# A Winograd convolution on one core: half of a late image stored by GpSimd's queue, one separate slice of rows given up, the first store issued by ScalarE

## The chip, the core and the metric

The kernel runs on one core of a Trainium2 chip. The metric is the device time in microseconds (us), the median of several runs. Lower is better. One further execution was profiled; all durations below come from it.

## The reference

A 3x3 convolution with padding 1 over 16 images of 64 channels and 64 x 64 pixels, giving 128 channels, all in float32:

```python
x_pad = np.pad(x, ((0, 0), (0, 0), (1, 1), (1, 1)), mode='constant')
# for every b, co, ci, kh, kw:
output[b, co] += weight[co, ci, kh, kw] * x_pad[b, ci, kh:kh+h, kw:kw+w]
```

The input x has 16.8 MB, the output 33.6 MB.

## The kernel before

Two images make a pair: their 2 x 64 input channels fill the 128 partitions. There are 8 pairs, p = 0 to 7, and each is worked in two halves of 32 output rows, h = 0 and 1 (line 185). GpSimd makes the Winograd row sums and differences of a half two steps ahead (line 206). TensorE multiplies (lines 216 to 228), ScalarE copies partial sums out of PSUM and casts input rows, and VectorE and ScalarE write the finished rows of the half into an output tile (lines 229 to 232).

Inputs and outputs live in nine slots of one tile, `homes`. Each slot holds one 2 MB block: the input of a pair, or one image of an output pair, in which each of the 128 partitions has 16 KB, one output channel. `X_HOME` and `O_HOME` (lines 49, 50) say which slots a pair takes. A slot is used again once the transfer that reads it has landed and the engines that read it are through.

All DMA transfers are issued from SyncE's queue (SP), in program order: the weights (line 58), the inputs of pairs 0 to 4 at the start (lines 68 to 72, pairs 3 and 4 in one transfer of 4 MB), then stores and the loads of pairs 5 to 7 in turn (lines 234 to 236). `store(p, both)` runs after the second half of a pair:

- for the pairs in `BOTH = (0, 3, 6)`, one transfer of 4 MB with both images (line 190);
- for the others, one transfer of 2 MB for each image (line 199);
- with `FEW = 5, 1, 7`, the second image of pair 5 goes in three: 57 rows of all 128 channels, and the last 7 rows as one transfer of 124 channels and one of 4 (lines 194 to 196).

`keep` holds the instructions of an engine in the order in which they are written. GpSimd has no compute after the transforms of the last half, and it issues no DMA.

Of the kernel before, what the change touches and what calls it, by code (L numbers as in the profile page):

```python
# [15 lines left out]
def kernel(  # L16
# [12 lines left out]
    nc = tc.nc  # L29
    B, CI, H, W = x.shape  # L30
    CO = weight.shape[0]
# [4 lines left out]
    keep = tc.keep_in_program_order  # L36
# [11 lines left out]

    X_HOME = [0, 1, 2, 7, 8, 2, 7, 8]
    O_HOME = [5, 3, 0, 5, 3, 0, 5, 2]  # L50
    BOTH = (0, 3, 6)
    FEW = 5, 1, 7
    NEXT_LOADS = {(2, 0): 5, (3, 0): 6, (4, 0): 7}
    homes = slots.tile([128, 9, H, W], F32)
    xs = [homes[:, k, :, :] for k in X_HOME]
# [4 lines left out]
    def load(p, cuts=((0, H),)):  # L60
        for lo, hi in cuts:
            keep(
                nc.sync.dma_start(
                    xs[p][:, lo:hi, :], x_rows[128 * p : 128 * p + 128, lo:hi, :]
                )
            )
# [55 lines left out]
    def cast(p, h):  # L122
        t = cpool.tile([128, 17, W], F16, tag="xh", name="xh")
        keep(nc.scalar.copy(t, xs[p][:, C_ROW[h] : C_ROW[h] + 17, :]))  # L124
        return t

    def transforms(eng, p, h):
        return sums(eng, p, h), diffs(eng, p, h), outers(eng, p, h)
# [17 lines left out]
    def mms(tiles, terms, start, stop):  # L146
        n = 3 * len(terms)
        i = 0
        for wi, src, row in terms:
            for kw in (1, 0, 2):  # L150
                c_lo, c_hi = max(0, 1 - kw), min(W, W + 1 - kw)
                lo, hi = 0, RB
                at, step, rows = row
                while at + step * lo < 0:
                    lo += 1
                while at + step * (hi - 1) > rows - 1:
                    hi -= 1
                first, last = at + step * lo, at + step * (hi - 1)
                for b2 in range(2):
                    p0 = 64 * b2  # L160
                    keep(
                        nc.tensor.matmul(  # L162
                            tiles[:, b2, lo:hi, c_lo:c_hi],
                            Wt[p0 : p0 + 64, wi, kw, :],
                            src[
                                p0 : p0 + 64,
                                first : last + 1 : step,
                                c_lo + kw - 1 : c_hi + kw - 1,
                            ],
                            start=start and i == 0,  # L170
                            stop=stop and i == n - 1,
                            skip_group_check=not start,
                        )
                    )
                i += 1

    def acc():
        return psum.tile([128, 2, RB, W], F32, tag="acc", name="acc")

    def copied(tiles):  # L180
        ut = upool.tile([128, 2, RB, W], F32, tag="ut", name="ut")
        keep(nc.scalar.copy(ut, tiles))  # L182
        return ut
# [3 lines left out]
    def store(p, both):  # L187
        if p in BOTH:
            pair = out[2 * p : 2 * p + 2, :, :, :].rearrange("b c h w -> c b h w")
            keep(nc.sync.dma_start(pair, both))  # L190
            return
        for b2 in range(2):
            parts = [(0, CO, 0, H)]
            if (p, b2) == FEW[:2]:
                at = H - FEW[2]
                parts = [(0, CO, 0, at), (0, 124, at, H), (124, 4, at, H)]
            for c, n, lo, hi in parts:
                keep(
                    nc.sync.dma_start(
                        out[2 * p + b2, c : c + n, lo:hi, :], both[c : c + n, b2, lo:hi, :]  # L200
                    )
                )

    for n, (p, h) in enumerate(halves):
        if n + 2 < len(halves):
            tr[halves[n + 2]] = transforms(nc.gpsimd, *halves[n + 2])
        if h == 0:
            both = homes[:, O_HOME[p] : O_HOME[p] + 2, :, :]
            ov = both.rearrange("p b (j i) c -> p b j i c", i=2)
        ss, dd, ee = tr.pop((p, h))  # L210
        xc = xh.pop((p, h))
        jf, jg = RB * F_BLK[h], RB * G_BLK[h]
        sf, sg = jf - 16 * h, jg - 16 * h
        g_at = 2 * jg - C_ROW[h]

        pf1, pg1, pf2, pg2 = acc(), acc(), acc(), acc()
        mms(pf1, [(HP, ss, (sf, 1, 16))], True, True)
        ux = copied(pf1)
        mms(pg1, [(G1, ss, (sg, 1, 16))], True, True)
        ug = copied(pg1)  # L220
        mms(pf2, [(HM, dd, (0, 1, RB))], True, True)
        uy = copied(pf2)
        if n + 1 < len(halves):
            xh[halves[n + 1]] = cast(*halves[n + 1])
        mms(pg2, [(G01, xc, (g_at, 2, 17)), (G2, xc, (g_at + 2, 2, 17))], True, True)
        mms(pf1, [(G0, ee, (0, 2, 16))], False, True)
        mms(pg1, [(G21, xc, (g_at + 1, 2, 17)), (G0, xc, (g_at - 1, 2, 17))], False, True)
        mms(pf2, [(G2, ee, (1, 2, 16))], False, True)
        keep(nc.vector.tensor_add(ov[:, :, jg : jg + RB, 1, :], pg2, ug))  # L229
        keep(nc.vector.tensor_add(ov[:, :, jf : jf + RB, 0, :], pf1, uy))  # L230
        keep(nc.vector.tensor_sub(ov[:, :, jf : jf + RB, 1, :], ux, pf2))  # L231
        keep(nc.scalar.copy(ov[:, :, jg : jg + RB, 0, :], pg1))  # L232
        if h == 1:
            store(p, both)
        if (p, h) in NEXT_LOADS:
            load(NEXT_LOADS[p, h])
# [30 lines left out]
```

## Time and profile before

| what | value |
|---|---|
| median of 3 runs | 127.05 us (126.71 to 127.71) |
| the profiled execution | 126.84 us |
| its span, from first to last instruction | 125.0 us |
| TensorE busy | 96.3 us (77%), done by 103.5 us |
| GpSimd, ScalarE, VectorE busy | 90.5, 81.5, 64.3 us |
| moved by DMA | 50.77 MB, mean 406 GB/s |
| HBM read, written | 17.07 MB, 33.55 MB |

The span is the stretch that the profile shows; the profiled execution's own time has some 1.8 us around it. In the profile PE is TensorE, DVE VectorE, ACT ScalarE, POOL GpSimd and SP SyncE; a "q" behind the name is the engine's issuing sequencer. Slices are fortieths of the span, 3.1 us each, and a digit is the busy share in tenths. L199 is line 199 of the kernel. The trace also has a record of each DMA packet, with its queue, its size, its start and its duration; a packet of 4 bytes is the count that a DMA engine adds to a semaphore when its part of a transfer is done. The records do not say which of the 16 DMA engines carried a packet.

### The profile page before, as it was taken

How to read it: one execution, taken by the hardware profiler on the slowest of the kernel's cores; microseconds unless marked ns; L12 is line 12 of the kernel's file. 1: busy time of each engine (PE TensorE's matmuls, PEld its weight loads, DVE VectorE, ACT ScalarE, POOL GpSimd, SP SyncE). 2: the span in 40 equal slices, each digit the busy share in tenths (PEclk: the TensorE clock that was granted, in tenths of full speed). 3: DMA queues.
4: the chain of work that ended last, by engine and by line, in shares of the span. 5: the costliest groups of instructions: out<-in, count | busy, mean ns of one | idle time of the engine just before them, and what ended most of it. 6: DMA issues, size and time to landing. Idle time of an engine off the chain costs nothing.

```text
span 125.0 us, 2161 instructions
## 1 busy us (share of the span) xinstructions
PE 96.3 (77%) x873; PEld 48.3 (39%) x873; DVE 64.3 (51%) x56; ACT 81.5 (65%) x86; POOL 90.5 (72%) x52
## 2 busy tenths in 40 slices
PE   0339999999999999999999999999999991000000
PEld 0213455554545545554545555545545540000000
DVE  0199484655738393947557483939374664000000
ACT  4456569789897979797888989797978842000000
POOL 2209999999999999999999999999999500000000
PEclk9999999999999999999999999999999999555555
DMA  4999999999999999999999999999999999999991
GB/s 126 364 433 440 430 430 430 425 346 404 430 425 419 440 430 440 406 425 425 432 438 398 430 425 425 435 430 425 430 419 428 428 421 431 435 425 440 430 388 63
DMA packets 3826, 50.77 MB, mean 406 GB/s; under 512 B 360, under 2 KB 488, under 8 KB 744
## 3 DMA queue, kind: packets, MB, share of 16 engines
q1 hardware_dynamic: 3816, 50.63, 96.6%
q8 instruction: 7, 0.11, 0.3%
q14 instruction: 3, 0.02, 0.1%
HBM read 17.07 MB, written 33.55 MB: 405 GB/s over the span
## 4 chain that ended last, share of the span: by engine, by line
PE 77%; DVE 3%; DMA 3%; POOL 1%; ACT 0%; issue 0%; DVEq 0%
PE acc L162 76%; DMA w_raw<-in_weight_dram 3%; DVE homes L231 1%; DVE ss L106 1%; POOL w L78 1%; DVE th L133 0%; DVE Wt L134 0%; PE wp L95 0%; ACT g0h L131 0%; DVEq L134 0%
## 5 line engine op out<-in xcount | busy, mean ns | idle before, releaser
L162 PEld LDWEIGHTS <-Wt 64*128 64x128 f16 x864 | 47.4, 96 | 50.0 <-issue 4.4
L182 ACT COPY ut<-acc 128x1024 f32<-128x1024 f32 x48 | 45.7, 1021 | 5.5 <-PE acc L162 5.5
L162 PE MATMUL acc<-xh,Wt 64*128 64x504 f16 (+3 forms) x384 | 46.9, 376 | 0.0
L106 POOL TENSOR_TENSOR ss<-homes 128x1024 f16<-128x1024 f32 x15 | 35.3, 2352 | 5.0 <-DMA homes<-in_x_dram 5.0
L229 DVE TENSOR_TENSOR homes<-acc,ut 128x1024 f32<-128x1024 f32 x16 | 19.6, 1225 | 32.4 <-PE acc L162 30.2
L119 POOL TENSOR_TENSOR ee<-homes 128x1024 f16<-128x1024 f32 x15 | 35.4, 2359 | 0.0
L162 PE MATMUL acc<-ss,Wt 64*128 64x504 f16 (+1 forms) x192 | 24.8, 392 | 2.4 <-DVE ss L106 2.4
L162 PE MATMUL acc<-ee,Wt 64*128 64x504 f16 (+1 forms) x192 | 26.3, 377 | 0.0
L232 ACT COPY homes<-acc 128x1024 f32<-128x1024 f32 x16 | 16.2, 1013 | 12.7 <-PE acc L162 12.0
L231 DVE TENSOR_TENSOR homes<-ut,acc 128x1024 f32<-128x1024 f32 x16 | 19.5, 1221 | 2.0 <-PE acc L162 1.3
L113 POOL TENSOR_TENSOR dd<-homes 128x512 f16<-128x512 f32 x15 | 20.0, 1332 | 0.0
L230 DVE TENSOR_TENSOR homes<-acc,ut 128x1024 f32<-128x1024 f32 x16 | 19.4, 1215 | 0.0
L124 ACT CAST xh<-homes 128x1088 f16<-128x1088 f32 x16 | 17.9, 1120 | 0.0
L162 PE MATMUL acc<-dd,Wt 64*128 64x504 f16 (+1 forms) x96 | 13.9, 392 | 0.0
L95 PE MATMUL wp<-ident,w 128*128 128x128 f16 x9 | 1.1, 309 | 4.8 <-POOL w L78 4.8
L133 DVE SCALAR_TENSOR_TENSOR th<-wp,g0h 128x384 f32<-128x384 f32 x1 | 0.6, 557 | 5.8 <-ACT g0h L131 5.8
L119 DVE TENSOR_TENSOR ee<-homes 128x1024 f16<-128x1024 f32 x1 | 2.9, 2866 | 0.0
L95 PEld LDWEIGHTS <-w 128*128 128x128 f16 x9 | 0.9, 158 | 4.7 <-POOL w L78 4.7
L78 POOL CAST w<-w_raw 128x576 f16<-128x576 f32 x1 | 0.7, 662 | 2.7 <-DMA w_raw<-in_weight_dram 2.7
L79 ACT CAST w<-w_raw 128x576 f16<-128x576 f32 x1 | 0.7, 671 | 1.9 <-DMA w_raw<-in_weight_dram 1.9
L79 ACT ACT_TABLE_LOAD x1 | 1.3, 1283 | 0.7 <-PEq L251 0.7
L106 DVE TENSOR_TENSOR ss<-homes 128x1024 f16<-128x1024 f32 x1 | 1.2, 1224 | 0.0
(15 smaller groups left out, 5.7 us busy)
## 6 DMA issues: line engine op xcount, KB each, us to landing
out_dram<-homes SPq DMA_DIRECT2D x9, 2048.0 KB, 16.7
out_dram<-homes SPq DMA_DIRECT2D x3, 4096.0 KB, 21.2
homes<-in_x_dram SPq DMA_DIRECT2D x5, 2048.0 KB, 19.0
homes<-in_x_dram SPq DMA_DIRECT2D x1, 4096.0 KB, 28.0
out_dram<-homes SPq DMA_DIRECT2D x1, 1824.0 KB, 22.6
homes<-in_x_dram SPq DMA_DIRECT2D x1, 1088.0 KB, 5.8
homes<-in_x_dram SPq DMA_DIRECT2D x1, 960.0 KB, 7.8
w_raw<-in_weight_dram SPq DMA_DIRECT2D x1, 288.0 KB, 3.2
```

The lines of the kernel that those rows point to most:

```text
L79: keep(nc.scalar.copy(w16[:, 1, :], w_raw))
L95: keep(nc.tensor.matmul(wps[kh][:, k * CO : k * CO + CO], w16[:, :, 3 * kh + k :: 9], ident))
L106: keep(eng.tensor_add(t, v[:, j : j + 16, 0, :], v[:, j : j + 16, 1, :]))
L113: keep(eng.tensor_sub(t, v[:, j : j + RB, 1, :], v[:, j : j + RB, 0, :]))
L119: keep(eng.tensor_sub(t, xs[p][:, r - 1 : r + 15, :], xs[p][:, r + 1 : r + 17, :]))
L124: keep(nc.scalar.copy(t, xs[p][:, C_ROW[h] : C_ROW[h] + 17, :]))
L162: nc.tensor.matmul(tiles[:, b2, lo:hi, c_lo:c_hi], Wt[p0 : p0 + 64, wi, kw, :], src[p0 : p0 + 64, first : last + 1 : step, c_lo + kw - 1 : ...
L182: keep(nc.scalar.copy(ut, tiles))
L229: keep(nc.vector.tensor_add(ov[:, :, jg : jg + RB, 1, :], pg2, ug))
L230: keep(nc.vector.tensor_add(ov[:, :, jf : jf + RB, 0, :], pf1, uy))
L231: keep(nc.vector.tensor_sub(ov[:, :, jf : jf + RB, 1, :], ux, pf2))
L232: keep(nc.scalar.copy(ov[:, :, jg : jg + RB, 0, :], pg1))
```

## The change

Four things change. The second image of pair 5 goes in one transfer, without the separate rows. Pair 3 leaves `BOTH` and goes as two transfers of one image each. Pair 0's store is issued by ScalarE in place of SyncE. For the last pair's first image, the upper 32 rows of channels 0 to 122 are issued by GpSimd, 3 channels (120 to 122) and then 120 (0 to 119), as soon as the pair's first half is computed; SyncE issues the same rows of the other 5 channels and then the lower 32 rows of all 128 after the second half, as before, and the second image after that.

```diff
-    BOTH = (0, 3, 6)
-    FEW = 5, 1, 7
+    BOTH = (0, 6)
+    SOFT = 7, 0, 32
...
-            keep(nc.sync.dma_start(pair, both))
+
+            eng = nc.scalar if p == 0 else nc.sync
+            keep(eng.dma_start(pair, both))
             return
         for b2 in range(2):
             parts = [(0, CO, 0, H)]
-            if (p, b2) == FEW[:2]:
-                at = H - FEW[2]
-                parts = [(0, CO, 0, at), (0, 124, at, H), (124, 4, at, H)]
+            if (p, b2) == SOFT[:2]:
+                parts = [(123, 5, 0, SOFT[2]), (0, CO, SOFT[2], H)]
...
+    def soft_store(p, both):
+
+
+        b2, hi = SOFT[1:]
+        for c, n in ((120, 3), (0, 120)):
+            keep(
+                nc.gpsimd.dma_start(
+                    out[2 * p + b2, c : c + n, 0:hi, :], both[c : c + n, b2, 0:hi, :]
+                )
+            )
...
         keep(nc.scalar.copy(ov[:, :, jg : jg + RB, 0, :], pg1))
+        if (p, h) == (SOFT[0], 0):
+            soft_store(p, both)
         if h == 1:
             store(p, both)
```

## The prediction

> **What bounds the kernel now.** I read the page's slices first, then the chain of waits, then SP's own waits and the timeline around each store, and last the DMA packet records.
>
> ```profile
> PE   0339999999999999999999999999999991000000
> ...
> DMA  4999999999999999999999999999999999999991
> GB/s 126 364 433 440 430 430 430 425 346 404 430 425 419 440 430 440 406 425 425 432 438 398 430 425 425 435 430 425 430 419 428 428 421 431 435 425 440 430 388 63
> ...
> q1 hardware_dynamic: 3816, 50.63, 96.6%
> q8 instruction: 7, 0.11, 0.3%
> ```
>
> TensorE is done after two thirds of the row; the DMA engines are full from the second slice to the last but one. Bytes over rate make the time: 50.63 MB at the usual 430 GB/s are 117.7 us of the 125.0 us span. The dent of 346 and 404 is in slices 8 and 9 (25 to 31 us).
>
> ```profile
> 8.31 95.19 PE acc L162 x864
> 103.50 0.02 issue
> 103.52 1.22 DVE homes L231
> ```
>
> The chain of waits ends with the last output tile at 104.74 us. SP issues the last two transfers then, and nothing but DMA is left:
>
> ```profile
> 24.26 0.39 SPq L190 DMA_DIRECT2D out_dram<-homes  x1
> ...
> 93.30 0.40 SPq L190 DMA_DIRECT2D out_dram<-homes  x1
> 104.80 1.92 SPq L199 DMA_DIRECT2D out_dram<-homes  x2
> ```
>
> At 104.80 us pair 6's 4 MB are still under way; its 16 parts land from 111.2 to 114.5 us. So compute has some 6 us of cover, and the end is set by the slowest of 16 DMA engines.
>
> Which engine that is can be rebuilt. An engine starts a packet 4 ns before the end of the one before is put down, and a 16 KB packet takes 611 ns, so the records string into 16 chains. Their last packets end at 120.5, 120.7, 121.0, 121.4, 122.1, 122.2, 122.3, 122.35, 122.4, 122.8, 123.1 (two), 123.3, 123.5, 123.6 and 123.9 us; the last count is seen 0.3 us later, at 124.2, and 0.8 us of closing instructions follow. The mean is 122.4: perfect balance would give 1.5 us, no more. Seven chains each carry one instruction packet (q8, some 0.95 us); the last chain has the first of them and besides a packet of 2089 ns in the dent. Four chains carry pair 5's 7 separate rows: 32 packets of 1792 bytes each. They end at 122.8, 123.1, 123.5 and 123.6; the last chain is none of the four.
>
> **The change part by part.** *Separate rows given up.* The four chains lose 32 packets at 74 ns less 3.5 overlap (2.26 us) and get 8 packets of 611 in place of 545 ns (0.53): 1.73 us less. The twelve others get 0.53 us more, among them the last one. Whatever else happens, the last chain goes from 123.9 to 124.4: **+0.53 us**, unless it is relieved. Two issues on SP fall away; SP waits for outputs, so that is nothing.
>
> *The half image on GpSimd's queue.* The transfer of 124 channels gives the nearest row for how channels spread: its packets lie in four chains, 31 channels each, and 4 is the largest divisor of 124 up to 16. (The 360 four-byte packets agree: 22 transfers with 16 counts, two with 4.) Read in that way, 120 channels go over 15 engines, 8 each, 3 over three and 5 over five. A packet of 8 KB, between 7680 bytes (291 ns) and 8704 (328), is 310 ns, net 306. Fifteen engines carry the same load as now (16 times 306 against 8 times 607: +0.04); the sixteenth is spared 8 times 306 = 2.45 us; some get one or two packets more, +0.31 each. What it does to the end depends on which engine is spared. If the last one: the next are those at 123.3 and 123.1, which end at 123.9 and 123.7, so −0.02 us in all. If any other: +0.57. The trace before has no transfer from GpSimd and the records name no engines, so both ends stay in the range. I take +0.57: fifteen engines of sixteen give it.
>
> [...]
>
> *Its timing.* The rows are final at 99.04 us (VectorE's L231 starts at 97.82 and takes 1.22). GpSimd's last work ends at 98.8, so nothing queues behind the two issues but the closing drain. Their making has no row; SP's take 0.33 to 1.5 us each. Against that stand 12 us until pair 6's parts land: nothing. The transfer takes turns with pair 6's packets, which land some 2.4 us later; nobody waits for them. If the second half's writes to the same slot waited for the transfer, the last issue would slip by some 8 us past its 6 us of cover; but pair 0's first half started at 7.04 us, while the second part of its load landed until 9.5, so waits go by rows: nothing. SP issues three transfers at the end in place of two, 0.4 us under the same cover.
>
> *First store on ScalarE.* ScalarE is between its copies of L232 and L182:
>
> ```profile
> 22.30 1.01 ACT L232 COPY homes<-acc 128x1024 f32<-128x1024 f32 x1 [0.62 <-PE acc L162]
> 23.60 2.84 ACT L182 COPY ut<-acc 128x1024 f32<-128x1024 f32 x3 [0.28 <-PE acc L162]
> ```
>
> It now waits for VectorE's L231 (until 24.17) and issues for 0.4: the next copies start at about 24.6, 1.0 us late, and 0.9 us of idle time in each half takes that up in about two. TensorE may slip by up to 1 us; the 6 us of cover hide it. On a second queue the store's packets take turns with the 4 MB load of pairs 3 and 4, which then lands up to 4 us later than its 31.3; GpSimd reads it at 39.98. The store frees its slots at about 42 to 44; VectorE writes there at 49.3. Both covers hold, and without them it would be TensorE that slips, under the same 6 us.
>
> What may move is the dent:
>
> ```profile
> 24.00:28.00 4.00, 4.00 (x40) 2.05 (x38) 1.91 (x3) 3.44 (x4) 4.00 (x3) 1.00 1.07 369
> 28.00:32.00 4.00, 4.00 (x42) 2.05 (x38) 1.90 (x3) 3.66 (x4) 4.00 (x4) 1.00 0.94 401
> ```
>
> The last two columns are DMA share and GB/s: engines busy, bytes few. The packets that start from 25 to 28 us run over by 0.83 us per engine. That is the gain's bound. Taking turns between loading and storing could also cost: crossings in the later loads cost 0.13 us per engine (67 to 69 us), and slices of 406 and 398 GB/s 0.2 us each. So −0.83 to +0.2. The dent comes with the first crossing from loading to storing, and that remains; I take **−0.2**, nearer to the small later crossings than to the whole dent gone.
>
> *Pair 3 in two transfers.* One issue more on SP (0.4 us, with a backlog of 17 us behind it) and 16 counts of 9 ns: nothing. Pair 6 writes into its slots at 83.8 us, and its last part lands at 81.0; a slip past 2.8 us would hold VectorE, again under the cover.
>
> **Sum.** 126.84 + 0.53 + 0.04 − 0.2 = **127.2 us**, from the profiled execution, which lies 0.2 below the median of 127.05.
>
> [...]
>
> **The rivals.** *The spared engine is the last one, and the dent goes* (faster): 126.84 − 0.02 − 0.83 = 126.0 us. For it: one engine with a known delay is just what a transfer over 15 can spare. Against it: one in sixteen by count, another chain comes 0.6 us behind, and the dent may be bound to the first write. With a little luck among the next chains, 125.6.
>
> *Packets of a second queue cost more* (slower). The one row of a second queue is q8: 16 KB in 0.95 us, where q1 needs 0.61. If GpSimd's packets ran so, 8 of them would take 8 times 0.17 = 1.35 us more on every engine: 126.84 + 0.57 + 1.35 = 128.8 us. From 0.09 us extra a packet it is slower by over 1%. Against it: q8 moves instructions, not output, and its neighbours in the chain run at 611 to 650 ns.
>
> *The 120 channels go over few engines.* Over 8 engines, 15 packets each in place of 8: 2.1 us more on these, 126.84 + 0.57 + 2.1 = 129.5 us. Against it: the row of the 124.
>
> **How the numbers follow.** Forecast, 126.7 to 127.7: 0.56. The faster rival with its halves (only the dent, or only the spared engine): 0.26; second queue dear: 0.13; few engines: 0.05. A measurement of this kernel (126.71 to 127.71 in three runs) tells about 1% from no change. Faster by over 1% (below 125.8) takes the faster rival's best part, 0.10; slower (above 128.3) most of the last two, 0.16; within, 0.74. The range from 125.8 to 128.6 leaves out 0.10 below, and above it about half of the dear queue and the few engines, 0.10.
>
> **What would show it.** The last chain: a spread of last landings as wide as now (3.3 us) with a late one says that another engine was spared; under 2.5 us, the right one. A row of GpSimd's queue among the DMA queues with 310 ns a packet, or with 475. Slices 8 and 9 near 430 say that the dent went. ScalarE's copy after the issue at about 24.6. I am wrong if VectorE waits for a DMA in the last half, if the DMA row has a gap before the end, or if the closing instructions grow beyond 0.8 us.

## The result and the profile after

The changed kernel takes 128.53 us (median of 7 runs, 127.97 to 128.62) against 127.05 us: 1.0106 times the time before, with a 95% interval of 1.0083 to 1.0128. It is slower by about 1%. A ratio, here and below, leaves out executions that took over 1.5% longer than the fastest of their kernel, so it differs a little from the quotient of the medians. The profiled execution took 128.62 us, its span is 126.8 us. The forecast was 127.2 us, the range 125.8 to 128.6.

The first view is the page of the changed kernel: the slices for TensorE, for the DMA engines' busy share and for the bytes, and the DMA queues.

```profile
PE   0339999999999999999999999999999920000000
...
DMA  4999999999999999999999999999999999999980
GB/s 117 390 454 434 424 424 434 434 315 429 455 408 424 419 444 424 416 424 437 439 411 408 439 439 429 419 424 444 424 429 419 429 434 369 367 341 398 431 377 36
...
q1 hardware_dynamic: 3434, 45.43, 86.2%
q10 hardware_dynamic: 272, 4.19, 7.8%
q0 software_dynamic: 176, 1.01, 2.3%
q8 instruction: 7, 0.11, 0.3%
```

Two queues are new: q10 is ScalarE's, with the 4.19 MB of pair 0, and q0 is GpSimd's, with 1.01 MB (123 channels of 8 KB). TensorE ends no later (102.3 us against 103.5). The DMA row is as full as before, with no gap ahead of the end. But from slice 33 to slice 36 the engines are busy and move only 369, 367, 341 and 398 GB/s, where the kernel before moved 425 to 440. Those slices, 104.6 to 117.3 us, hold most of GpSimd's transfer, whose packets run from 103.3 to 114.9 us. Its issue, in the timeline of GpSimd, and SP's last issues:

```profile
98.50 1.21 POOL L211 DMA_DIRECT2D out_dram<-homes  x2
```

```profile
97.92 8.62 SPq L200 DMA_DIRECT2D out_dram<-homes  x3
```

SP's first issue, of the 5 channels, goes out at 97.92 us, as soon as the upper rows are final (97.85 us); it does not wait for the second half.

The windows give the same loss as rates. A row has the stretch and its length, the busy time of PE, PEld (weight loads), DVE, ACT and POOL, and the granted clock of TensorE. The columns that matter are the last two, DMA share and GB/s; the changed kernel first, then the kernel before.

```profile
100.00:103.00 3.00, 2.29 (x22) 0.98 (x18) 2.83 (x3) 1.08 (x2) 0.00 (x0) 1.00 1.02 431
103.00:112.50 9.50, 0.00 (x0) 0.00 (x0) 0.55 (x1) 0.00 (x0) 0.00 (x0) 0.72 1.01 369
112.50:120.00 7.50, 0.00 (x0) 0.00 (x0) 0.00 (x0) 0.00 (x0) 0.00 (x0) 0.50 0.99 402
```

```profile
100.00:103.00 3.00, 3.00 (x32) 1.55 (x30) 2.00 (x2) 1.33 (x3) 0.00 (x0) 1.00 0.99 418
103.00:112.50 9.50, 0.48 (x6) 0.00 (x0) 1.57 (x2) 0.94 (x1) 0.00 (x0) 0.68 1.01 430
112.50:120.00 7.50, 0.00 (x0) 0.00 (x0) 0.00 (x0) 0.00 (x0) 0.00 (x0) 0.50 1.02 435
```

Summed over the packet records, the changed kernel had moved 41.18 MB by 100 us, 0.14 MB more than the kernel before; by 115 us it had moved 46.94 MB, 0.50 MB less. The 0.64 MB lost in between are 1.5 us at 0.43 MB per us. The 16 engines' last counts say the same: their mean went from 122.7 to 124.1 us, the last from 124.2 to 125.9 us. So nearly all of it is a loss of rate on all engines, not a longer tail of one. In GpSimd's 123 packets the median is close to the forecast 310 ns, 309 ns, but 35% are slow (over it by more than 5%), up to 1294 ns, and the mean is 381.

### The profile page after: what moved, and what is told of

Its sections match the earlier page's. It is cut to its first block, busy times and chain, and to the rows that moved or that the text cites. A ratio compares the mean times of both kernels' runs of the same rounds, so it can differ in the third digit from the quotient of the medians.

```text
span 126.8 us, 2163 instructions
## 1 busy us (share of the span) xinstructions
PE 95.1 (75%) x873; PEld 50.5 (40%) x873; DVE 63.8 (50%) x56; ACT 81.4 (64%) x86; POOL 91.7 (72%) x54
## 3 DMA queue, kind: packets, MB, share of 16 engines
q10 hardware_dynamic: 272, 4.19, 7.8%
q0 software_dynamic: 176, 1.01, 2.3%
## 4 chain that ended last, share of the span: by engine, by line
PE 74%; DVE 3%; DMA 3%; POOL 1%; ACT 0%; issue 0%; DVEq 0%
PE acc L162 74%; DMA w_raw<-in_weight_dram 3%; DVE homes L243 1%; DVE ss L106 1%; POOL w L78 1%; DVE th L133 0%; DVE Wt L134 0%; PE wp L95 0%; ACT g0h L131 0%; DVEq L134 0%
## 5 line engine op out<-in xcount | busy, mean ns | idle before, releaser
L162 PEld LDWEIGHTS <-Wt 64*128 64x128 f16 x864 | 49.6, 95 | 46.4 <-issue 2.9
L162 PE MATMUL acc<-xh,Wt 64*128 64x504 f16 (+3 forms) x384 | 46.0, 370 | 0.0
```

What stands on the lines that cost most here:

```text
L162: nc.tensor.matmul(tiles[:, b2, lo:hi, c_lo:c_hi], Wt[p0 : p0 + 64, wi, kw, :], src[p0 : p0 + 64, first : last + 1 : step, c_lo + kw - 1 : ...
```

## The experiments

Three theories could explain the loss. *Dear queue*: GpSimd's transfers cost rate. *Split*: the odd numbers of channels do it, on any queue. *Turn-taking*: any second queue beside SP's does it. Times are medians; each ratio is to the kernel before on the same chip, with its 95% interval.

**Without the half image on GpSimd's queue** (`no_soft`)

```diff
-    SOFT = 7, 0, 32
+    SOFT = -1, 0, 32
```

> The changed kernel without the half image on GpSimd's queue: the last pair's first image goes in one transfer on SP. The dear-queue theory (GpSimd's transfer lowers the rate of all 16 DMA engines while it runs, 1.5 us lost from 103 to 115 us) and the split theory (it is the odd split of channels that costs, on any queue) both expect the dip to 369 GB/s after 103 us to vanish and the time to fall by about 1.5 us, to 127.0. The rival that the loss comes from the other three edits, above all the rows given up, expects 128.0 or more.

Measured: 127.28 us, ratio 1.0033 (1.0006 to 1.0060), and no dip:

```profile
103.00:112.50 9.50, 0.00 (x0) 0.00 (x0) 0.05 (x1) 0.00 (x0) 0.00 (x0) 0.69 1.01 431
```

The dip and most of the excess belong to the half image. The other three edits together leave 0.3%.

**The same split on ScalarE's queue** (`soft_act_3_120`)

```diff
-                nc.gpsimd.dma_start(
+                nc.scalar.dma_start(
                     out[2 * p + b2, c : c + n, 0:hi, :], both[c : c + n, b2, 0:hi, :]
```

> The same two transfers of 3 and 120 channels at the same place, issued by ScalarE in place of GpSimd. Dear-queue theory: no dip, packets of 8 KB at 309 ns, 126.8 to 127.3. Split theory (15 engines with 8 channels each read across the usual groups of partitions and get in each other's way): dip stays, 128.3 to 128.7. Turn-taking theory (any second queue beside SP's costs): dip stays too.

Measured: 129.08 us, ratio 1.0185 (1.0098 to 1.0272). Four executions give a wide interval, and the median lies above the 128.7 us that the split theory named. The 123 packets have a mean of 359 ns, up to 1112. The window of this kernel:

```profile
103.00:112.50 9.50, 1.27 (x12) 0.45 (x8) 2.61 (x3) 1.03 (x2) 0.00 (x0) 0.82 1.01 375
```

The dip is there without GpSimd. The dear queue, the first reading of the profile after, falls.

**All 128 channels on GpSimd's queue, and on ScalarE's** (`soft_gp_128`, `soft_act_128`)

```diff
-                parts = [(123, 5, 0, SOFT[2]), (0, CO, SOFT[2], H)]
+                parts = [(0, CO, SOFT[2], H)]
...
-        for c, n in ((120, 3), (0, 120)):
+        for c, n in ((0, CO),):
```

The second has `nc.scalar.dma_start` besides.

> The half image on GpSimd's queue as one transfer of all 128 channels, none on SP. Dear-queue theory: the dip to about 370 GB/s stays, mean packet about 380 ns, 128.3 to 128.8. Split theory: the dip goes, 127.0 to 127.4.

> The half image on ScalarE's queue as one transfer of all 128 channels. Dear-queue and split theories: no dip, 127.0 to 127.4. Turn-taking theory: dip, 128 or more.

Measured: 127.49 us, ratio 1.0045 (1.0008 to 1.0083) by GpSimd, and 127.32 us, ratio 1.0053 (1.0022 to 1.0084), by ScalarE. Against 1.0033 without any half image neither queue costs anything that these runs resolve. The page's queue row and the window of the kernel with GpSimd's 128 channels, then the window of the one with ScalarE's:

```profile
q0 software_dynamic: 144, 1.05, 2.0%
```

```profile
103.00:112.50 9.50, 0.01 (x1) 0.00 (x0) 1.22 (x1) 0.47 (x1) 0.00 (x0) 0.63 1.01 429
```

```profile
103.00:112.50 9.50, 0.38 (x4) 0.00 (x0) 1.72 (x2) 0.84 (x1) 0.00 (x0) 0.65 1.01 429
```

By GpSimd it is more bytes in less time than in the changed kernel (1.05 MB in 2.0% against 1.01 in 2.3%), and no dip. In both kernels all but one or two packets in a hundred take 309 ns. Turn-taking falls too: GpSimd's transfer took turns with SP's from 103.6 to 112.5 us. The profiled execution of the ScalarE kernel was the longest of its ten, 129.03 us; there is no dip in it, and what is late is one engine, to which the last section comes back.

**Other splits over all 16 engines** (`soft_act_112_16`, `soft_act_64_64`)

```diff
-        for c, n in ((0, CO),):
+        for c, n in ((112, 16), (0, 112)):
```

The other kernel has `((0, 64), (64, 64))`. Both take ScalarE's queue. The *divisor rule* is a reading of the counts here: a transfer of SP's queue goes over as many engines as the largest divisor of its channels up to 16. In the kernel before, 124 channels give 4 counts and lie in four chains, and 128 give 16; in the changed kernel SP's 5 channels give 5 (357 four-byte packets on q1, from 22 transfers with 16 counts and this one). By it 16 and 112 channels go over all 16 engines, 1 and 7 each; for these splits, and on ScalarE's queue, that is an estimate.

> The half image on ScalarE's queue in transfers of 16 and 112 channels, none on SP. [...] Alignment theory (engines slow each other when their channels do not fall in the groups that the 128-channel transfers use): dip after 103 us, 8 KB packets above 340 ns, 128.3 or more. Fifteen-engine theory (only uneven loads cost): no dip, 309 ns, 127.2 to 127.5.

> The half image on ScalarE's queue in two transfers of 64 channels, each 4 channels on each of 16 engines by the divisor rule. [...] If only odd counts of channels cost: no dip, 127.2 to 127.5.

Measured: 128.10 us, ratio 1.0076 (1.0041 to 1.0110), for 16 and 112, a little under the 128.3 that the alignment theory named, and 128.28 us, ratio 1.0099 (1.0065 to 1.0133), for 64 and 64. Mean packets are 411 and 403 ns, with 36% and 35% of them slow. The windows, 112 and 16 first:

```profile
103.00:112.50 9.50, 1.13 (x12) 0.34 (x6) 2.47 (x3) 1.01 (x1) 0.00 (x0) 0.76 1.01 372
```

```profile
103.00:112.50 9.50, 1.59 (x16) 0.58 (x11) 2.94 (x3) 1.35 (x2) 0.00 (x0) 0.80 1.00 365
```

By that estimate no engine is spared here and the load is even, 8 packets each, yet the dip stays (372 and 365 GB/s). So, as far as the estimate holds, it is not the number of engines, and it is not an odd count: 64 is as even as 128. Nor is it that two transfers stand in the queue in place of one: the 16 channels are done by 104.0 us, and of the 107 packets that start after that, with the 112 channels alone in the queue, 41 are slow. Only the transfer of all 128 channels runs at full rate beside the others (429 GB/s in the window by either queue). That the split slows the engines is thus shown; why it does is not. Which channels an engine carries the records do not show, so the alignment theory stays a guess. The runs agree with it as far as every split tried here is slow, apart from the 124 channels of the kernel before (74 ns for every packet). A rival stays open: the splits also change which parts of HBM are written at the same time, and no run separates the two ends of the transfer.

**A split of 120 in order on one queue** (`few_120`)

```diff
-    FEW = 5, 1, 7
+    FEW = 5, 1, 24
...
-            keep(nc.sync.dma_start(pair, both))
+            eng = nc.scalar if p == 0 else nc.sync
+            keep(eng.dma_start(pair, both))
...
-                parts = [(0, CO, 0, at), (0, 124, at, H), (124, 4, at, H)]
+                parts = [(0, CO, 0, at), (0, 120, at, H), (120, 8, at, H)]
```

> The kernel before with pair 0's store on ScalarE, and pair 5's second image as 40 rows of 128 channels, then 24 rows of 120 channels and of 8, all on SP. The 120 lie in order behind 128-channel transfers, nothing takes turns with them. Turn-taking together with alignment as the cause: no dip, 6 KB packets near 232 ns. Alignment alone: slow packets in this transfer too. One engine is spared 24 rows of 8 channels (1.8 us): if it is the one that ends last, the time falls to about 126.0; if it is another, it rises by 0.5 us to 127.2 (twelve engines no longer relieved by the 4-engine transfer).

Measured: 128.67 us, ratio 1.0121 (1.0068 to 1.0173). The 6 KB packets have a median of 234 ns and a mean of 264, with up to 896: slow packets without a second queue beside them. Strung into chains, the records show eight chains with nine of these packets, seven with eight, and one with none, as the divisor rule has it for 120 and 8 channels. The spared chain ends at 122.1 us, the last at 125.3. Sparing an engine works, but this was not the one that ended last. The time is 1.5 us above the higher of the two expectations. The slow 6 KB packets are 0.24 us of it per engine; the two last chains end 1.1 us behind the next, and why they do is open.

**One edit alone** (`few_off`, `first_act`, `soft_only`)

```diff
-    FEW = 5, 1, 7
+    FEW = -1, 1, 7
```

> The kernel before, with only the separate rows of pair 5 given up. The prediction's term: the last engine's chain gets 0.53 us more, 127.5 to 127.6. If the last engine is another one in most executions, 127.0 to 127.2.

Measured: 127.43 us against 126.98, ratio 1.0033 (0.9998 to 1.0069). The median is 0.45 us up, between the two expectations and near the term of 0.53, but the interval just includes no change.

```diff
-            keep(nc.sync.dma_start(pair, both))
+            eng = nc.scalar if p == 0 else nc.sync
+            keep(eng.dma_start(pair, both))
```

> The kernel before, with only pair 0's store issued by ScalarE. The prediction's term: 0.2 us less, 126.8 to 126.9, with the dent at 25 us a little smaller. If the dent belongs to the first crossing from loads to stores, it stays and the time is 127.0 to 127.1.

Measured: 126.70 us against 126.98, ratio 0.9993 (0.9960 to 1.0026): no change that can be told. From 24 to 28 us it moves 377 GB/s against 369 before and 344 in the changed kernel. The dent stays, and it did not depend on whose queue the store was in.

For the third, `SOFT` and its code were added to the kernel before, with `FEW`, `BOTH` and SP's first store kept:

```diff
     BOTH = (0, 3, 6)
     FEW = 5, 1, 7
+    SOFT = 7, 0, 32
...
+            if (p, b2) == SOFT[:2]:
+                parts = [(123, 5, 0, SOFT[2]), (0, CO, SOFT[2], H)]
...
+        if (p, h) == (SOFT[0], 0):
+            soft_store(p, both)
```

> The kernel before, with only the half image on GpSimd's queue (3 and 120 channels there, 5 on SP); the separate rows stay, pair 0 goes by SP. Dear-queue theory: 1.5 us more for the lost rate, 128.3 to 128.7, with a dip after 103 us. The prediction's own term without a dear queue: 127.1.

Measured: 131.09 us, ratio 1.0290 (1.0223 to 1.0357). By the ratio the half image costs 3.7 us here, more than any theory expected. The page shows a deeper dip:

```profile
GB/s 146 359 457 427 433 433 433 407 331 433 433 422 422 443 427 415 427 427 425 433 415 433 422 427 433 412 443 433 417 436 425 420 414 305 369 303 397 427 275 31
```

42% of GpSimd's packets are slow, against 35%, and the mean of the last counts is 125.3 us.

**The separate rows and 128 channels together** (`soft_rows_128`). The kernel just shown, with the split changed to 128 channels as in `soft_gp_128`, and pair 0's store on ScalarE.

> The kernel before with pair 0's store on ScalarE and the half image on GpSimd's queue as one transfer of 128 channels; pair 5's separate rows and pair 3's single transfer stay. Alignment theory: GpSimd's queue costs nothing when the channels lie in the usual groups, the relief of the separate rows stays: 126.6 to 127.1, 8 KB packets at 309 ns. If the 131.1 of the half image beside the separate rows came from those two together, whatever the split: 128.5 or more, with slow packets.

Measured: 126.79 us against 127.16, ratio 0.9986 (0.9959 to 1.0014). Packets of 309 ns, and the window is as it was before the change:

```profile
103.00:112.50 9.50, 0.32 (x4) 0.00 (x0) 1.41 (x2) 0.78 (x1) 0.00 (x0) 0.67 1.02 432
```

GpSimd's queue and the separate rows get along. It takes the split to make the 3.7 us. Why the split costs so much more beside the separate rows is not settled. In the trace of `soft_only` the four chains with the separate rows each take one of SP's 5 channels as well, 0.3 us, and end at 125.6, 125.9, 127.2 and 127.4 us; that is a part, and the rest is open. This kernel and `first_act` are the best of all here; neither can be told from the kernel before.

## Why the prediction was partly right

*That DMA sets the end, and compute does not:* right. The changed kernel's TensorE ends before 103 us, and the DMA row has no gap. VectorE's one wait put down to a DMA, 2.2 us before 94.2, is as long as its waits for TensorE at this place in other halves. The closing instructions after the last count take 0.89 us against 0.83, nothing beside the 1.5.

*Separate rows given up, +0.53 us:* the size was right, 0.45 in the medians, on the edge of what the runs resolve. The chains of `few_off` agree: as in the kernel before, the one with the first instruction packet ends last, at 124.2 in place of 123.9 us.

*The half image, "Fifteen engines carry the same load as now":* this is the step that failed. It priced a packet by its size alone, 310 ns from the rows of 7680 and 8704 bytes, which all come from transfers of 128 channels. The nearest row for a split, the 124 channels on four engines, stood at 74 ns for every packet and gave no warning. With 3 and 120 channels the mean is 381 ns, and SP's 16 KB packets beside them are slowed too: those that start from 103 to 113 us run over by 0.90 us per engine. Together with 8 times 72 ns on GpSimd's own packets, 0.58 us, that is 1.5 us, the loss that the bytes show.

*Which engine is spared:* one count stands 1.7 us ahead of the next where the last half image lands (116.2 against 117.9 us) and 0.8 ahead at the end, so an engine was spared, and not the last one: choosing +0.57 over −0.02 was right. Nor was it one of the four with the separate rows: in `soft_only`, where the rows stay and GpSimd's transfers are the same, the chain without GpSimd's packets has none of them. The chain that ended last is a slow one of which the prediction says nothing; the last section has it.

*First store on ScalarE, −0.2:* as a time not resolved: the interval of `first_act`, 0.9960 to 1.0026, holds it as well as nothing. The dent from which it was to come stays with either queue (0.78 us per engine in `first_act`, 0.83 before), so it belongs to the first crossing or to something else in that stretch. The delay was as worked out. In the timeline ScalarE's copies after its issue lose 1.1 us more than usual (idle 1.40 against 0.28) and catch up within two halves:

```profile
23.00 0.42 ACTq L192 DMA_DIRECT2D out_dram<-homes  x1
23.46 2.84 ACT L182 COPY ut<-acc 128x1024 f32<-128x1024 f32 x3 [1.40 <-PE acc L162]
26.18 1.12 ACT L124 CAST xh<-homes 128x1088 f16<-128x1088 f32 x1
27.18 1.04 ACT L244 COPY homes<-acc 128x1024 f32<-128x1024 f32 x1
```

*The rival of the dear second queue, 128.8 us:* its number came out, its mechanism did not. The packets did get longer by 72 ns, just under the 0.09 us that it named, but GpSimd's queue runs at full rate with 128 channels (429 GB/s in the window), ScalarE's at a loss with 3 and 120 (375). Its row, q8, spoke of instruction packets and not of queues. Which engine issues the half image made no difference that these runs resolve: 127.28, 127.49 and 127.32 us for the same bytes from SP, GpSimd and ScalarE.

*The sum:* 126.84 + 0.57 + 1.5 = 128.9 us for the profiled execution, which took 128.62. The chance given to slower by over 1% was 0.16, and the measured 1.06% lies just beyond that bound. That 128.53 us falls inside the range is luck: the range reached up to 128.6 us for the dear queue and the few engines, and neither is what happened.

## What to carry to other kernels

Where all DMA engines are full, price a transfer by how its channels are split, not only by bytes and queue: a store of part of the 128 partitions, put beside stores of all 128, cost 1.5 us here for 1 MB. If a piece has to be cut off, cut it along the rows and keep 128 partitions; here either queue then ran at full rate (429 GB/s). And before balancing the engines, string the packets into chains and see which one ends last, and whether the same one does so in the next execution.

## What the runs showed that was not expected

- A split into two transfers of 64 channels is as slow as 3 and 120, or slower: mean packets of 403 and 359 ns on the same queue, against 312 for 128 channels.
- The 124 channels on four engines have packets of 1792 bytes at 74 ns, without exception, in the kernel before. Why these escape is open.
- One engine seems to be slow in every kernel, the one before included. In each trace 66 to 85 packets of 16 KB between 28 and 103 us take 637 to 699 ns in place of 611. In nine of the 13 traces 62 to 75 of them string into one chain, without an instruction packet, and cost it 2.4 to 2.8 us; in the other four they lie mainly on two. Before the change this chain ends at 123.1 us. In the changed kernel it takes one of SP's 5 channels besides and ends last, at 125.6 us, 0.8 behind the next; in `soft_gp_128` and `soft_act_128` it is last by 1.5 and 2.3 us. Why this engine is slow is open.
- All seven instruction packets lie on different chains, one each, about 14 us apart, and in `first_act` and the kernel before never on the four that carry the separate rows.
- A dent at 24 to 28 us, 0.5 to 0.9 us per engine, is in every trace, with the first store on either queue.
